# Fused substitution steps, joint weight-tile factors and a new instruction order in a one-core hybrid encoder kernel

## The chip, the cores and the metric

The kernel runs on one core of one Trainium2 chip. The metric is the device time of one execution in microseconds (us). Five engines work side by side, each through its own list of instructions in a fixed order: TensorE (PE in the profile; PEld are its weight loads), VectorE (DVE), ScalarE (ACT), GpSimd (POOL) and SyncE (SP), which issues the DMA transfers. An engine waits when the next instruction in its list needs something that another engine hasn't finished.

## The reference

One layer of an encoder trunk, over a prompt of 2048 frames and a second sequence of 32 frames with caches; the model is 1024 wide. Both sequences go through the same steps:

```python
h = layer_norm(x)
qa, ka, va, za, qkv_b, zb, a_b, b_b, gate_a, gate_b = split(h @ w_in)
ya = (band_attention(qa, ka, va, rel_bias) * silu(za)) @ w_branch_a      # 8 heads of 64, band of 9 chunks of 64
q, k, v = split(silu(causal_conv(qkv_b, conv_w)))                        # width 4
ob, state = gated_delta_rule(l2(q) / 8, l2(k), v, g(a_b), sigmoid(b_b), state)
yb = (rms_norm(ob) * gdn_norm_w * silu(zb)) @ w_branch_b
y = layer_norm(ALPHA * h + (sigmoid(gate_a) * ya + sigmoid(gate_b) * yb) @ w_out)
```

The delta rule runs over chunks of 64 frames. For each chunk and head a unit lower triangular system has to be inverted, and the state is carried from chunk to chunk:

```python
m = (k_beta @ k.T) * decay * strict                   # strictly lower triangular, 64x64
t_inv = triangular_solve(eye + m, eye)                # lower, unit diagonal
u, w = t_inv @ v_beta, t_inv @ (k_beta * exp(gc))
v_new = u - w @ s                                     # the chain: each chunk needs the state s before it
o = (q * exp(gc)) @ s + qk @ v_new
s = s * exp(g_last) + k_dec.T @ v_new
```

## The kernel before

The prompt is worked on in two halves of 1024 frames; the 32 sampled frames go along with the second. Each half has a delta-rule stage (branch B, `phase_b`) and an attention stage (branch A, `phase_a`); the branch products, the merge and the output projection come after, in part beside the second attention stage. Heads are taken in pairs of 128 partitions.

**Projections.** `w_in` is cut into 49 tiles of 128 columns. A tile is fetched (`wraw`), scaled by a power of two found from its squares, and divided into two half-precision parts (`whi`, `wlo`); `h` is kept in the same way (`hi`, `lo`). A projection block `pj` is 8 + 8 + 8 matmuls of 512 or 272 columns into one of two PSUM banks, and an eviction by ACT or DVE frees the bank (`raw`, `zb`, `vf`, `sig` and others). Since the scaling has to be undone, `factors` computes two numbers per tile, `w_inv` and `w_half`, from `w_scale` on DVE; evictions read them as scalars.

**Delta stage.** A half has 8 blocks (4 head pairs, twice 8 chunks), the second half one more for the sampled frames: 17 systems. For each block DVE and ACT compute a convolution (`acc` from `raw`, or from `raws` for the sampled frames), norms and decays; `system` makes the matrices `p_c` (the masked products, times the factor `e_p`) on PE and DVE; `solve` sends their 32x32 diagonal blocks through DRAM into `sys_p`, 128 systems side by side on the partitions, and `substitute` inverts them on DVE in 31 steps: step j takes column j times the rows known so far (`sys_t`) and subtracts it (`sys_u`). Only rows j // 4 + 1 of 8 are touched, so early steps are short. Two solvers run at a time. `inverse` brings the result back (`tu`, `tu_t`) and fills in the off-diagonal 32x32 blocks with matmuls (`z_c` between them). The state chain (`chain`) then takes for each chunk: PE x<-state, DVE r, PE x<-r, DVE vn, PE x<-vn, DVE state; beside it PE makes o<-state and o<-vn, which ACT copies into `v_t`. `tail` norms and gates a finished block (`sqo`, `ms`, `gb`) and stores it (`g`).

**What sets the order.** The program is written by generators, one for each stream of work. A planner (`Flow`) runs the one whose clock is earliest, and every instruction is appended to its engine's list as it is called. `Engine.price` gives each instruction a duration, `Flow.spend` books it: an engine is taken from its last booking, or a hop after the stream's last step, whichever is later (0.10 us into PE, 0.12 us on the same engine, 0.20 us between others). So the numbers in `price` decide the order of all five lists, and where among the projections the steps of the chain lie. On the chip there is no planner: the lists are fixed, and only semaphores hold an engine back.

Every instruction of the planned engines is recorded at one line, that of the call inside `Engine` (L267 before, L279 after), so the profile is read by names of tiles, not by lines. The lines of the old planner that the change touches:

```python
if a[1].dtype == F16:
    return max(n / 2400.0, m / 4800.0)
if a[1].dtype == F32R:
    return n / 2400.0
return max(n, m) / (1200.0 if name == "transpose" else 600.0)
...
return (0.05 if far else 0.093) + 0.093 * more + n / 1200.0
...
return (0.125 if far else 0.068) + 0.06 * more * fast + n / (1920.0 if fast else 960.0)
```

Here n is the width in elements, m that of the stationary operand, `far` is true where an operand lies in PSUM, `more` counts operands that are read as one scalar per partition, and `fast` is true for copies and TENSOR_SCALAR in SBUF. The last two lines are ACT and DVE.

## Time and profile before

| | before |
|---|---|
| median of 3 runs | 1968.77 us (1964.63 to 1972.47) |
| the profiled execution | 1967.06 us |
| its span, first to last instruction | 1965.2 us |
| PE busy | 1894.8 us (96%) |
| DVE busy | 1409.0 us (72%) |
| ACT busy | 993.6 us (51%) |
| POOL busy | 771.2 us (39%) |
| mean granted PE clock | 0.989 |
| DMA queue, share of 16 engines | 51.9% |

PE's busy time is a union of its matmuls, whose ends are modelled and which overlap, so 96% says that PE hardly stands still, not that it runs at its peak. DVE's share is an average: the profile's slices show it at 7 to 9 tenths in the delta stages, which lie at about 98 to 491 us and 884 to 1277 us, and at 4 to 7 tenths for most of the rest.

The kinds of rows that are read below: a row of a wait names the engine and the tile that waited, what was waited for, the time in total, the number of waits and the longest; a row of a group has the busy time and the mean duration in ns behind the bar, and then the idle time before it; a row in order of time has its start and its length in us.

### The profile page before, as it was taken

What the parts mean: (1) busy time and instruction counts of PE and PEld (TensorE: products, weight loads), DVE (VectorE), ACT (ScalarE), POOL (GpSimd) and SP (SyncE); (2) the same over time, 40 slices, a digit from 0 to 9 for tenths busy, and PEclk for the clock granted to TensorE, in tenths of its full rate; (3) what the DMA queues carried; (4) which work ended last, traced back from release to release, by engine and by line L of the source; (5) the groups of instructions that cost most, each with busy time, mean ns of one, the idle gap of its engine ahead of it and who ended that gap; (6) DMA issues with size and microseconds to landing.
All of it is one profiled execution on the core that took longest, in us unless ns stands there. A gap on an engine that the chain in (4) does not pass through costs nothing. (4 is left out here: it accounts for less than half of the span.)

```text
span 1965.2 us, 40968 instructions
## 1 busy us (share of the span) xinstructions
PE 1894.8 (96%) x14513; PEld 1339.0 (68%) x14513; DVE 1409.0 (72%) x4401; ACT 993.6 (51%) x2022; POOL 771.2 (39%) x1079
## 2 busy tenths in 40 slices
PE   8999999999999998999999999999999999999998
PEld 5445666676455556666776777768877667988886
DVE  7689989973378768679898987355556565465797
ACT  6665545544586777565544444354446575321110
POOL 7344334433344445444344333422222233243673
PEclk9999999999999999999999999999999999999999
DMA  3234232333368887223233233477878798996552
GB/s 134 69 89 114 78 108 68 84 90 105 115 154 203 179 185 168 75 81 84 58 79 93 67 91 103 120 206 189 223 190 172 184 198 187 263 331 200 179 183 89
DMA packets 382950, 274.61 MB, mean 140 GB/s; under 512 B 248339, under 2 KB 319359, under 8 KB 382745
## 3 DMA queue, kind: packets, MB, share of 16 engines
q1 hardware_dynamic: 382744, 272.00, 51.9%
q8 instruction: 114, 1.87, 0.4%
q14 instruction: 92, 0.75, 0.1%
HBM read 157.15 MB, written 71.76 MB: 116 GB/s over the span
## 5 line engine op out<-in xcount | busy, mean ns | idle before, releaser
L267 PE MATMUL pj<-hi,whi 128*128 128x512 f16 (+2 forms) x1992 | 643.0, 338 | 11.6 <-DVE zb L267 3.1
L267 PE MATMUL pj<-hi,wlo 128*128 128x512 f16 (+2 forms) x1952 | 634.5, 338 | 0.6 <-POOL wlo L267 0.5
L267 PEld LDWEIGHTS <-whi 128*128 128x128 f16 x3984 | 408.8, 104 | 229.0 <-issue 9.6
L267 POOL TENSOR_TENSOR wlo<-wraw,whi 128x256 f16<-128x256 f32 (+1 forms) x392 | 281.4, 740 | 466.9 <-ACT whi L267 380.7
L267 PE MATMUL pj<-lo,whi 128*128 128x512 f16 (+2 forms) x1992 | 453.0, 338 | 0.0
L267 PEld LDWEIGHTS <-wlo 128*128 128x128 f16 x1952 | 204.9, 105 | 116.2 <-issue 13.2
L267 ACT ACTIVATE sb<-sb,mx,unit 128x640 f32<-128x640 f32 (+4 forms) x128 | 108.6, 849 | 101.1 <-DVE mx L267 96.0
L267 POOL TENSOR_TENSOR pu<-sb,pu 128x640 f16<-128x640 f32 (+2 forms) x64 | 82.2, 1284 | 177.6 <-ACT pu L267 135.5
L267 ACT ACTIVATE wraw<-wraw,w_scale 128x1024 f32<-128x1024 f32 (+1 forms) x98 | 111.4, 1137 | 78.1 <-DVE w_scale L267 75.8
L267 ACT CAST whi<-wraw 128x512 f16<-128x512 f32 (+2 forms) x212 | 128.2, 611 | 28.0 <-PE pj L267 24.9
L267 DVE TENSOR_TENSOR sys_u<-sys_u,sys_t 128x60 f32<-128x60 f32 (+24 forms) x527 | 124.8, 242 | 5.7
L267 DVE SCALAR_TENSOR_TENSOR acc<-raw,cwT,acc 128x512 f32<-128x512 f32 x144 | 112.4, 781 | 7.9 <-ACT acc L267 6.5
L267 DVE TENSOR_TENSOR sys_t<-sys_u,sys_p 128x60 f32<-128x60 f32 (+21 forms) x459 | 110.6, 244 | 5.5
L267 ACT CAST mh<-sf 128x256 fp32r<-128x256 f32 x64 | 25.7, 406 | 158.3 <-PE c L267 78.1
L267 ACT COPY v_t<-o 128x64 f32<-128x64 f32 x132 | 27.7, 210 | 142.1 <-PE o L267 105.5
L267 DVE CUSTOM_DVE_ANT_0 sb<-a,bias 128x320 f32<-128x320 f32 (+5 forms) x136 | 66.2, 498 | 45.1 <-PE a L267 42.5
L267 POOL TENSOR_TENSOR w_scale<-w_scale,mhalf 128x1 f32<-128x1 f32 x49 | 32.0, 652 | 155.7 <-DVE w_scale L267 118.0
L267 PE MATMUL b<-ghi,whi 128*128 128x256 f32 (+1 forms) x320 | 89.3, 311 | 1.2 <-DVE cr L267 1.1
L267 POOL TENSOR_TENSOR ml<-sf,mh 128x256 fp32r<-128x256 f32 x60 | 59.5, 993 | 77.3 <-PE c L267 51.5
L267 ACT ACTIVATE sig<-pj,w_half 128x512 f32<-128x512 f32 (+2 forms) x84 | 49.3, 587 | 75.7 <-PE pj L267 70.3
L267 ACT CAST pu<-sb 128x640 f16<-128x640 f32 (+4 forms) x128 | 82.2, 650 | 0.7
L267 PEld LDWEIGHTS <-pt 128*128 128x128 f16 x1680 | 65.8, 98 | 23.3 <-issue 6.0
(389 smaller groups left out, 4202.9 us busy)
## 6 DMA issues: line engine op xcount, KB each, us to landing
wraw<-in_w_in SPq DMA_DIRECT2D x192, 256.0 KB
sf<-sig SPq DMA_DIRECT2D x112, 128.0 KB
sig<-sig SPq DMA_DIRECT2D x44, 256.0 KB
sg<-sig SPq DMA_DIRECT2D x37, 256.0 KB
sig<-sg SPq DMA_DIRECT2D x37, 256.0 KB
sys_p<-sol_p SPq DMA_DIRECT2D x68, 128.0 KB
x<-in_x_p SPq DMA_DIRECT2D x16, 512.0 KB
xt<-in_x_p SPq DMA_DIRECT2D x16, 512.0 KB
```

Source lines behind the costliest of these rows:

```text
L267: r = f(*a, **k)
```

## The change

There are four parts.

1. `Engine.price` gets other numbers. On PE half-precision matmuls cost 2.5 ns more, F32R ones some 5% and 6 ns more, and full-precision ones of 64 columns 0.168 us instead of 0.213. On ACT, operations of 1024 elements and half-precision ones out of PSUM on 64 partitions cost 0.13 us more. On DVE bn_aggr costs 0.16 more, TENSOR_TENSOR out of PSUM or on the substitution's rows 0.035 more, SCALAR_TENSOR_TENSOR of 512 elements 0.06 more in SBUF and 0.05 less out of PSUM. Nothing of this is executed; it moves instructions.
2. In `substitute`, steps with fewer than four rows use one SCALAR_TENSOR_TENSOR for each row (multiply by a scalar, then add, in place) instead of a multiplication into `sys_t` and a subtraction over all rows. All steps add instead of subtracting.
3. The sign that this needs is put into `e_p`, whose multiplication becomes a SCALAR_TENSOR_TENSOR with the constant -1; in turn `z_c` is a plain copy.
4. `w_inv` and `w_half` become the two columns of one tile `w_both`, written by one TENSOR_SCALAR (the two constants of `h_scale` times the reciprocal `w_one`) instead of two.

```diff
             if a[1].dtype == F16:
-                return max(n / 2400.0, m / 4800.0)
+                return max(n / 2400.0, m / 4800.0) + 0.0025
             if a[1].dtype == F32R:
-                return n / 2400.0
-            return max(n, m) / (1200.0 if name == "transpose" else 600.0)
+                return n / 2300.0 + 0.006
+            if name == "transpose":
+                return max(n, m) / 1200.0 + 0.002
+            if m <= 32:
+                return 0.064 + n / 1200.0 * (n > 32)
+            return max(n / 600.0, 0.112) + 0.006 + 0.05 * (n == HD)
...
-            return (0.05 if far else 0.093) + 0.093 * more + n / 1200.0
+            wide = 0.13 if n == KD * P or far and out.dtype == F16 and out.shape[0] == HD else 0.0
+            return (0.05 if far else 0.093) + 0.093 * more + n / 1200.0 + wide
...
+        if name == "tensor_tensor":
+            cost += 0.035 if far or len(out.shape) > 2 and out.shape[-1] < 32 and out.shape[0] == P else 0.0
+        if name == "scalar_tensor_tensor" and n == 512:
+            cost += -0.05 if far else 0.06
...
-        inv, half_ = w_inv[:, wid:wid + 1], w_half[:, wid:wid + 1]
-        V.reciprocal(out=half_, in_=w_scale[:, wid:wid + 1])
+        one = w_one[:, wid:wid + 1]
+        V.reciprocal(out=one, in_=w_scale[:, wid:wid + 1])
         yield
-        V.tensor_scalar(out=inv, in0=half_, scalar1=h_scale[:, 2:3], scalar2=None, op0=ALU.mult)
-        V.tensor_scalar(out=half_, in0=half_, scalar1=h_scale[:, 3:4], scalar2=None, op0=ALU.mult)
+        V.tensor_scalar(out=w_both[:, wid], in0=h_scale[:, 2:4], scalar1=one, scalar2=None, op0=ALU.mult)
...
-            V.tensor_tensor(out=e_p[:, 0:nch], in0=e_in[:, 0:nch], in1=bcast(s_p, nch), op=ALU.mult)
+            V.scalar_tensor_tensor(out=e_p[:, 0:nch], in0=e_in[:, 0:nch], scalar=-1.0, in1=bcast(s_p, nch),
+                                   op0=ALU.mult, op1=ALU.mult)
...
-                if nr == 1:
-                    V.tensor_scalar(out=sys_t[:, 0, 0:w], in0=sys_p[:, j, j + 1:32], scalar1=sys_u[:, 0, j:j + 1],
-                                    scalar2=None, op0=ALU.mult)
-                else:
-                    V.tensor_tensor(out=sys_t[:, 0:nr, 0:w], in0=sys_u[:, 0:nr, j:j + 1].to_broadcast([P, nr, w]),
-                                    in1=sys_p[:, j:j + 1, j + 1:32].to_broadcast([P, nr, w]), op=ALU.mult)
+                if nr < 4:
+                    for r in range(nr):
+                        u = sys_u[:, r, j + 1:32]
+                        V.scalar_tensor_tensor(out=u, in0=sys_p[:, j, j + 1:32], scalar=sys_u[:, r, j:j + 1], in1=u,
+                                               op0=ALU.mult, op1=ALU.add)
+                    yield
+                    continue
```

**DVE, the first steps of a substitution.** The first system's steps from a width of 31 columns on, before:

```order
L267 TENSOR_SCALAR sys_t<-sys_p,sys_u 128x31
L267 TENSOR_TENSOR sys_u<-sys_u,sys_t 128x31
L267 TENSOR_SCALAR sys_t<-sys_p,sys_u 128x30
L267 TENSOR_TENSOR sys_u<-sys_u,sys_t 128x30
L267 TENSOR_SCALAR sys_t<-sys_p,sys_u 128x29
L267 SCALAR_TENSOR_TENSOR acc<-raw_1426,cwT,acc 128x512
L267 TENSOR_TENSOR sys_u<-sys_u,sys_t 128x29
```

and with the change (x2 means two such rows in a line):

```order
L279 SCALAR_TENSOR_TENSOR sys_u<-sys_p,sys_u 128x31
L279 SCALAR_TENSOR_TENSOR acc<-raw_1437,cwT,acc 128x512
L279 SCALAR_TENSOR_TENSOR sys_u<-sys_p,sys_u 128x30
L279 SCALAR_TENSOR_TENSOR acc<-raw_1437,cwT,acc 128x512
L279 SCALAR_TENSOR_TENSOR sys_u<-sys_p,sys_u 128x29
L279 TENSOR_TENSOR sc<-gcb,col 128x8
L279 SCALAR_TENSOR_TENSOR sys_u<-sys_p,sys_u 128x28
L279 TENSOR_SCALAR ss<-b 64x8 x2
L279 SCALAR_TENSOR_TENSOR sys_u<-sys_p,sys_u 128x27 x2
```

One row stands for what were two, and from 27 columns on two or three rows for two; the 512-wide convolution steps of other streams now lie between them.

**PE, one step of the state chain.** Chunk step 65 (counted from 0 over both halves), the projections (`pj`) between x<-r and x<-vn, before:

```order
L267 MATMUL x<-r,u_bd_9736 128x64
L267 LDWEIGHTS wlo
L267 MATMUL pj<-hi_9067,wlo 128x512
L267 MATMUL o<-state,q_bd_9730 128x64
L267 LDWEIGHTS whi
L267 MATMUL pj<-hi_9067,whi 128x512
L267 MATMUL x<-vn,kd_bd_9733 128x64
```

and with the change:

```order
L279 MATMUL x<-r,u_bd_9692 128x64
L279 LDWEIGHTS whi
L279 MATMUL pj<-hi_9039,whi 128x512
L279 MATMUL o<-state,q_bd_9686 128x64
L279 LDWEIGHTS wlo
L279 MATMUL pj<-hi_9039,wlo 128x512
L279 LDWEIGHTS whi
L279 MATMUL pj<-lo_9040,whi 128x512
L279 LDWEIGHTS whi
L279 MATMUL pj<-lo_9040,whi 128x512
L279 MATMUL x<-vn,kd_bd_9689 128x64
```

Four projections stand where two stood.

**DVE, in front of one eviction.** The ninth eviction of a 512-wide `zb` block, which frees a projection bank early in the second half, before:

```order
L267 TENSOR_TENSOR q_bd_9731<-qk_10219,ex 64x8x64
L267 TENSOR_TENSOR sys_u<-sys_u,sys_t 128x6x10
L267 SCALAR_TENSOR_TENSOR acc<-raws_10830,cwT,acc 128x32
L267 TENSOR_TENSOR q_bd_9731<-qk_10219,ex 64x8x64
L267 TENSOR_TENSOR sys_t<-sys_u,sys_p 128x6x9
L267 SCALAR_TENSOR_TENSOR acc<-raws_10830,cwT,acc 128x32
L267 SCALAR_TENSOR_TENSOR zb<-zb,pj 128x512
```

and with the change:

```order
L279 SCALAR_TENSOR_TENSOR acc<-raw_10818,cwT,acc 128x512
L279 TENSOR_TENSOR sys_t<-sys_u,sys_p 128x6x8
L279 TENSOR_TENSOR kd_bd_9690<-b,sc 64x4x64
L279 SCALAR_TENSOR_TENSOR acc<-raw_10818,cwT,acc 128x512
L279 TENSOR_TENSOR sys_u<-sys_u,sys_t 128x6x8
L279 TENSOR_TENSOR kd_bd_9690<-b,swap 64x4x64 x2
L279 SCALAR_TENSOR_TENSOR acc<-raw_10818,cwT,acc 128x512
L279 TENSOR_TENSOR sys_t<-sys_u,sys_p 128x7x7
L279 SCALAR_TENSOR_TENSOR zb<-zb,pj 128x512
```

The q_bd steps and the convolution of the sampled frames have gone from in front of it, and the three steps of a 512-wide convolution and three kd_bd steps stand there.

17 lines of the change are left out of this document (11 added, 6 removed).

## The prediction

> **What bounds the kernel now.** I read the page's busy times first, then the stretches of the span, then what the matmul engine waited for.
>
> ```profile
> span 1965.2 us, 40968 instructions
> PE 1894.8 (96%) x14513; PEld 1339.0 (68%) x14513; DVE 1409.0 (72%) x4401; ACT 993.6 (51%) x2022; POOL 771.2 (39%) x1079
> ```
>
> PE is busy for 1894.8 of 1965.2 us. The change leaves PE's own work alone (the same matmuls but for three more warm-up ones on ones at the start), so only the 70.4 us in which PE stands still, and the clock it gets, can be won. The columns here are the stretch, its length, then each engine's busy time (instructions), then PE's clock and the DMA share.
>
> ```profile
> 0.00:40.00 40.00, 31.42 (x165) 17.92 (x165) 31.06 (x105) 23.96 (x50) 26.14 (x36) 0.91 0.44 153
> 98.00:293.00 195.00, 184.42 (x1277) 115.36 (x1276) 172.08 (x596) 108.73 (x207) 82.66 (x146) 0.98 0.35 98
> 293.00:491.00 198.00, 193.68 (x1512) 132.98 (x1513) 147.24 (x597) 93.40 (x199) 74.97 (x121) 1.00 0.31 86
> 491.00:884.00 393.00, 381.41 (x2856) 224.65 (x2855) 265.47 (x819) 275.40 (x521) 167.47 (x233) 1.00 0.60 145
> 884.00:1081.00 197.00, 186.94 (x1558) 136.55 (x1555) 179.26 (x640) 97.04 (x211) 76.44 (x140) 0.97 0.30 79
> 1081.00:1277.00 196.00, 191.92 (x1697) 146.48 (x1697) 139.71 (x557) 84.77 (x201) 69.14 (x114) 1.00 0.35 95
> 1277.00:1670.00 393.00, 384.08 (x3454) 292.66 (x3453) 229.27 (x709) 217.27 (x443) 112.27 (x121) 1.00 0.80 194
> 1867.00:1965.00 98.00, 90.09 (x392) 71.50 (x390) 83.57 (x106) 9.90 (x30) 53.18 (x52) 0.98 0.41 136
> ```
>
> PE's idle time is length minus PE busy: 8.6 us in the start, 29.1 in the two delta-rule halves (10.6 + 4.3 + 10.1 + 4.1), 20.5 in the two attention stages (11.6 + 8.9), 7.9 at the end; the rest, 4.1, is in stretches not shown. In the first part of each half DVE is busy for 172.08 of 195 and 179.26 of 197 us: it is the engine that PE waits for there.
>
> ```profile
> PE x L267 <- DVE vn L267: 6.1, 16, 0.8
> PE c L267 <- DVE ob L267: 4.6, 5, 1.4
> PE b L267 <- ACT p_c L267: 3.8, 2, 3.2
> PE x L267 <- DVE r L267: 3.7, 11, 1.1
> PE pj L267 <- DVE zb L267: 3.1, 1, 3.1
> PE o L267 <- ACT v_t L267: 2.7, 6, 0.7
> PE x L267 <- DVE sys_u L267: 1.8, 2, 1.1
> PE b L267 <- DVE kd_bd L267: 1.5, 1, 1.5
> PE b L267 <- POOL v_t L267: 1.5, 2, 1.4
> PE x L267 <- DVE state L267: 1.1, 4, 0.5
> ```
>
> No wait is longer than 3.2 us; these rows alone hold fifty. The recurrent chain (the rows of x and o) makes 6.1 + 3.7 + 2.7 + 1.8 + 1.1 = 15.4 us. The other rows of the delta halves (p_c, zb, kd_bd, v_t on POOL) make 3.8 + 3.1 + 1.5 + 1.5 = 9.9 us.
>
> **How such a wait arises.** One of them, in order of time (start, length in us):
>
> ```profile
> 951.15 0.67 DVE L267 TENSOR_TENSOR q_bd<-qk,ex 64x512 f32<-64x512 f32 x1
> 951.75 0.66 DVE L267 TENSOR_TENSOR sys_u<-sys_u,sys_t 128x28 f32<-128x28 f32 x1
> 952.33 0.27 DVE L267 TENSOR_SCALAR vn<-x,sc 128x64 f32<-128x64 f32 x1
> 952.66 0.43 PE L267 MATMUL x<-vn,kd_bd 128*128 128x64 f32 x2 [0.33 <-DVE vn L267]
> ```
>
> PE had two projection matmuls to do between x<-r and x<-vn; DVE had q_bd and a sys_u step in front of vn, and that sys_u took 0.66 us where its group's mean is 0.24 (row below). So part of a wait is a plan that is too tight, and part a duration that no fixed number foresees. The change can only reach the first.
>
> **The chain's order.** At the place shown in the section on the change, x<-r to x<-vn holds four projections instead of two. Counted over all steps, that hop holds 4.6 projections on average instead of 3.3, and at most three of them in 70 of 128 steps instead of 85 of 126. The other hops hardly change: state to r, at most three in 67 instead of 64; vn to state, 86 instead of 96. So short hops fall from 245 to 223, by a tenth, and by a fifth on the hop that waits most. Eight projections of this width take 1.89 us here, 0.22 us each:
>
> ```profile
> 1264.98 1.89 PE L267 MATMUL pj<-lo,whi 128*128 128x512 f16 x8
> ```
>
> Waits grow with the shortage, so I take a third of the chain's 15.4 us, **5 us**; bounds 0 and 12.
>
> **The other waits in the delta halves.** The dearer numbers for wide DVE and ACT operations push the planner to start dependants later. But in front of zb the new DVE order holds three 512-wide acc steps instead of two short ones, so this wait may well return. I take 40% of 9.9 us, **4 us**; bounds 0 and 8.
>
> **Attention stages.** Numbers of ACT casts and of DVE evacuations change by 0.05 to 0.13 us, and the order with them; of 20.5 us I take **3 us**; bounds -5 (new waits) and 10. Start and end keep their order nearly: **0**.
>
> **The substitution steps.**
>
> ```profile
> L267 DVE TENSOR_TENSOR sys_u<-sys_u,sys_t 128x60 f32<-128x60 f32 (+24 forms) x527 | 124.8, 242 | 5.7
> L267 DVE TENSOR_SCALAR sys_t<-sys_p,sys_u 128x31 f32<-128x31 f32 (+1 forms) x68 | 19.8, 291 | 0.3
> L267 DVE SCALAR_TENSOR_TENSOR acc<-raws,cwT,acc 128x32 f32<-128x32 f32 x36 | 10.4, 288 | 2.3 <-ACT acc L267 1.9
> L267 DVE SCALAR_TENSOR_TENSOR qk_s<-e,acc 128x32 f32<-128x32 f32 x8 | 1.5, 186 | 0.6 <-ACT e L267 0.6
> L267 DVE TENSOR_SCALAR w_inv<-w_half,h_scale 128x1 f32<-128x1 f32 x49 | 10.0, 204 | 0.5
> ```
>
> In each of 17 systems the first twelve steps lose 24 instructions (4 TENSOR_SCALAR, 20 TENSOR_TENSOR) and gain 24 fused ones (4 + 4 x 2 + 4 x 3), at most 31 wide. Removed: 4 x 0.291 + 20 x 0.242 = 6.0 us a system. Added: by the nearest row of the same kind (acc on raws, 32 wide, a scalar read per partition, adding in place) 24 x 0.288 = 6.9 us; by qk_s, whose scalar is a constant, 24 x 0.186 = 4.5 us. So DVE gains 1.5 us or loses 0.9 us per system, over 17 systems 26 us won to 15 us lost. I take the acc row, being the same form, less the overlap of rows that don't wait for each other: about nothing. The joint factor saves one 128x1 TENSOR_SCALAR for each of 49 tiles, 10.0 us of DVE by its row. The turned sign in e_p and the plain copy of z_c stay in instructions that were there. DVE isn't the bound, so none of it is PE time by itself: **0**.
>
> **The clock.** After some waits PE gets half its clock for one or two periods:
>
> ```profile
> core 0: 1965.2 us, clock 0.989
> 136.90:140.00 3.10, 0.01 (x1) 0.02 (x1) 3.06 (x11) 2.63 (x6) 3.10 (x3) 1.00 0.02 6
> 142.10:145.50 3.40, 3.40 (x11) 1.60 (x10) 3.32 (x13) 0.00 (x0) 0.99 (x1) 0.50 0.43 136
> 168.80:170.30 1.50, 0.20 (x1) 0.00 (x0) 1.44 (x4) 1.11 (x3) 0.36 (x1) 1.00 0.10 37
> 172.80:176.20 3.40, 3.40 (x11) 1.72 (x10) 3.02 (x19) 2.76 (x4) 2.91 (x3) 0.51 0.00 0
> ```
>
> A stop of 3.1 us at 137 and one of 1.3 us at 169 are each followed by 3.4 us at half clock, which costs 1.7 us of work. The mean clock of 0.989 makes some 20 us lost in all. If about two such periods go with the waits, **4 us**; bounds -3 and 10. The Trainium skill (TensorE: Matmul & The Clock Gate, "Why this matters for your kernels") advises against idle gaps over about 3 us; by that rule only the longest waits cost clock, this term would be under 2 us, and the sum 2 us less. The row at 172.8, behind a gap of 1.3 us, speaks against so high a threshold.
>
> **The ends of the halves.** The chain now ends nearer to the attention's first projection: 32 instead of 98 wide projections stand between them in the first half, and some 6.9 instead of 18.0 us of them in the second (6 and 48 of 512 and 272 columns, instead of 32 and 96). What follows the chain there now:
>
> ```profile
> 1241.47 0.33 PE L267 MATMUL o<-vn,qk_bd 128*128 128x64 f32 x2
> 1255.80 1.25 SPq L290 DMA_DIRECT2D g<-gb  x2
> 1266.90 0.69 ACT L267 ACTIVATE vf<-pj,w_inv 128x512 f32<-128x512 f32 x1 [3.53 <-PE pj L267]
> ```
>
> The last block's norm, gate and store end at 1257.1, 15.3 us behind the chain, and the first eviction of attention at 1266.9. With 11 us less between them that tail would end some 1 to 2 us after the eviction could begin; the second bank covers most of it: **-1 us**.
>
> **The sum.** 5 + 4 + 3 + 0 + 4 - 1 = 15 us. The profiled execution took 1967.06 us, 1.9 more than its span and 1.7 less than the median of 1968.77. So 1967 - 15 = **1952 us**. With the upper bounds (12 + 8 + 10 + 10) it would be 1927.
>
> **The rivals.** *The waits move.* Waits by scatter (the sys_u of 0.66 us) stay as many and stand elsewhere. For it: fifty small waits, short hops down by only a tenth, and the old order's luck is lost with its faults. Against it: the hop that waits most is the one that was widened. Time 1967, give or take 6.
>
> *DVE falls behind: slower.* The planner charges a fused step of 31 columns 0.10 us and a hop of 0.12 to the next on the same engine, 0.22. If on the chip each holds DVE for the whole 0.288 us of the acc row, it lags 24 x 0.07 = 1.6 us a system, 28 us in all, where DVE has only 23 and 18 us to spare in the first parts of the halves, and every chain step queues behind it. If half of it reaches PE and the other gains fail, 1967 + 14 = 1981. It decides once a fused step holds DVE for more than about 0.25 us. Against it: two or three fused steps in a row don't wait for each other, and above vn and the next acc start 0.20 us apart though vn takes 0.27, so independent instructions overlap.
>
> **How the numbers follow.** A measurement of this kernel can tell about 0.5% from no change. Forecast (some waits go) 0.53; waits move 0.31; DVE falls behind 0.16. Hence faster by over 0.5% 0.53, within it 0.31, slower 0.16. The range runs from 1932, near the upper bounds of the gains, to 1977, which leaves out the worse half of the slow case.
>
> **What would show it.** Right: PE idle near 59 us instead of 70, the waits for vn and r below 7 us together (now 9.8), the mean clock at 0.99 or above, PE's busy time shorter by the clock term alone. The fused steps: their row's mean between 0.19 and 0.29 us; above it the slow case. The second half's end: a wait of pj for vf near its end. Wrong: the same idle sum under other names, or idle grown most where DVE was fullest, after 98 and after 884 us.

## The result and the profile after

The changed kernel takes 1978.43 us (median of 6 runs, 1975.52 to 1982.23), the kernel before 1967.91 us in the runs beside it (6 runs, 1964.63 to 1972.47). The ratio is 1.0054, 95% interval 1.004 to 1.0067: slower by half a per cent where 0.8% faster was forecast. In a second measurement of the same kernel (e10 below) it was 1.0038 [1.0025, 1.0051]. The profiled execution took 1975.9 us, its span 1974.1 us, 8.9 more than before, at a mean clock of 0.987 (0.989 before).

The head of the page of the changed kernel:

```profile
span 1974.1 us, 40895 instructions
PE 1884.3 (95%) x14516; PEld 1344.8 (68%) x14516; DVE 1403.9 (71%) x4352; ACT 990.8 (50%) x2022; POOL 768.8 (39%) x1079
```

PE's idle time rose from 70.4 to 89.8 us, its busy time fell by 10.5. The stretches, with the columns of before (stretch, length, busy time of PE, PEld, DVE, ACT and POOL, PE clock, DMA share and rate):

```profile
0.00:40.00 40.00, 29.42 (x168) 17.28 (x168) 34.43 (x102) 22.38 (x47) 25.86 (x36) 1.00 0.41 141
40.00:98.00 58.00, 55.02 (x331) 30.36 (x332) 35.15 (x74) 37.58 (x62) 23.47 (x34) 0.94 0.21 68
98.00:293.00 195.00, 184.74 (x1263) 113.67 (x1262) 171.80 (x577) 109.60 (x208) 89.00 (x149) 0.98 0.35 97
293.00:491.00 198.00, 193.11 (x1542) 136.25 (x1542) 147.90 (x589) 95.21 (x203) 71.64 (x117) 1.00 0.31 87
491.00:884.00 393.00, 376.12 (x2817) 222.17 (x2816) 261.81 (x804) 270.51 (x515) 163.90 (x230) 0.99 0.60 145
884.00:1081.00 197.00, 188.42 (x1635) 143.33 (x1633) 179.05 (x635) 98.89 (x216) 76.77 (x140) 0.98 0.30 82
1081.00:1277.00 196.00, 192.28 (x1703) 148.93 (x1702) 140.91 (x571) 85.19 (x199) 72.11 (x121) 0.99 0.35 97
1277.00:1670.00 393.00, 379.03 (x3389) 286.99 (x3387) 229.10 (x703) 216.28 (x445) 110.73 (x121) 0.99 0.79 191
1670.00:1769.00 99.00, 89.10 (x728) 82.19 (x726) 50.99 (x92) 30.82 (x63) 32.48 (x31) 0.95 0.91 283
```

Length less PE busy: the delta halves stand still for 27.5 us (10.3 + 4.9 + 8.6 + 3.7; 29.1 before), the attention stages for 30.9 (16.9 + 14.0; 20.5 before), the start for 10.6 + 3.0 (8.6 + 0.2 before), and 1670 to 1769, where the merge begins, for 9.9 (3.0 before). So by idle time the loss isn't where DVE is fullest, but where the forecast expected little or nothing. What PE waited for (waiting tile, what was waited for, us in total, number, longest):

```profile
PE c L279 <- DVE ob L279: 9.3, 4, 6.6
PE b L279 <- ACT whi L279: 7.3, 5, 3.2
PE x L279 <- DVE r L279: 5.3, 8, 2.4
PE x L279 <- DVE vn L279: 4.8, 9, 0.8
PE pj L279 <- ACT part L279: 3.8, 1, 3.8
PE a L279 <- ACT mh L279: 3.7, 1, 3.7
...
PE pj L279 <- DVE zb L279: 1.1, 2, 0.9
```

Before, no wait was longer than 3.2 us. Now ob has one of 6.6, part one of 3.8 and mh one of 3.7, none of them in a delta half (that of part is at the opening of the second attention stage). The waits for r and vn are 10.1 us together (9.8 before), zb's fell from 3.1 to 1.1.

**A better measure than idle time.** PE's idle time misses part of what PE loses, as these rows in order of time show (changed kernel; start, length):

```profile
622.66 0.38 PE L279 MATMUL pj<-lo,whi 128*128 128x512 f16 x1
622.88 0.38 PE L279 MATMUL pj<-hi,whi 128*128 128x512 f16 x1
```

Each record lasts 0.38 us, but the next matmul starts after 0.22. A matmul that starts 0.16 us late leaves no idle time at all. So I took, for every matmul, the time to the start of the next one, less the median of that spacing in the kernel before, taken where two matmuls of its kind (same tiles, same shape) follow each other. The medians add up to 1773.0 us in both kernels (warm-up matmuls left out), so PE's own work is the same, and what is left over is called lost time. Its level hangs on this choice: with medians over all successors, a change from one kind to another counts as work, PE's own work is 1835.0 us, and 62 us less is lost in every kernel. The differences between kernels stay the same within 0.1 us.

The table adds the lost time up over the matmuls, cut at 65, 410, 780, 1122 and 1495 us of PE work, so that the same work is compared; the kernel before gets there at 96, 491, 881, 1277 and 1670 us, the edges of its stages. One profiled execution each, ratios from all runs of a kernel against before; cells are us lost. The column of the chains is the work from 150 to 440 and from 840 to 1120 us (193 to 521 and 951 to 1275 us in the kernel before), which holds nearly all steps of the state chains and leaves out the first part of each half. The us that the expectations of e5 and e16 to e18 give for the delta halves are of this last kind.

| run | ratio, 95% interval | start | half 1 | att. 1 | half 2 | att. 2 | merge, end | all | halves 1 + 2 | chains |
|---|---|---|---|---|---|---|---|---|---|---|
| before | 1 | 31.2 | 49.3 | 20.6 | 53.5 | 20.2 | 9.1 | 183.9 | 102.8 | 82.6 |
| changed | 1.0054 [1.0040, 1.0067] | 37.0 | 44.0 | 27.0 | 43.0 | 27.1 | 14.8 | 192.8 | 87.0 | 71.4 |
| e10 changed, again | 1.0038 [1.0025, 1.0051] | 37.3 | 41.5 | 26.9 | 42.7 | 28.9 | 16.1 | 193.4 | 84.2 | 71.6 |
| e1 new prices only | 1.0015 [1.0004, 1.0027] | 36.0 | 42.5 | 30.6 | 33.9 | 31.0 | 15.1 | 189.1 | 76.4 | 61.2 |
| e2 edits, old prices | 1.0000 [0.9987, 1.0013] | 32.2 | 59.4 | 21.1 | 53.1 | 15.9 | 12.4 | 194.0 | 112.5 | 94.9 |
| e3 edits, order held | 1.0033 [1.0020, 1.0046] | 30.0 | 52.8 | 17.7 | 58.8 | 19.5 | 9.3 | 188.0 | 111.6 | 93.3 |
| e4 new order, old steps | 1.0135 [1.0119, 1.0152] | 36.1 | 53.3 | 28.7 | 50.8 | 27.9 | 15.5 | 212.3 | 104.1 | 86.3 |
| e5 new prices in delta halves | 0.9967 [0.9955, 0.9979] | 34.6 | 48.9 | 24.9 | 37.2 | 26.9 | 11.1 | 183.5 | 86.1 | 69.5 |
| e6 new prices elsewhere | 1.0110 [1.0092, 1.0129] | 31.5 | 60.7 | 21.7 | 56.0 | 23.7 | 14.9 | 208.6 | 116.7 | 100.1 |
| e7 = e5 with the edits | 0.9965 [0.9950, 0.9980] | 32.3 | 46.4 | 22.1 | 42.6 | 23.2 | 10.5 | 177.1 | 89.0 | 75.4 |
| e8 prices of PE only | 1.0074 [1.0049, 1.0100] | 34.6 | 54.5 | 27.1 | 44.8 | 24.6 | 9.4 | 195.1 | 99.3 | 78.9 |
| e9 = e7, gate blocks later | 0.9980 [0.9967, 0.9993] | 34.0 | 44.9 | 27.6 | 41.0 | 20.7 | 10.9 | 179.1 | 85.9 | 73.5 |
| e11 before, LEAD nudged | 1.0006 [0.9995, 1.0017] | 30.0 | 53.0 | 22.3 | 51.0 | 18.1 | 10.5 | 184.9 | 104.0 | 83.6 |
| e12 before, hop nudged | 1.0014 [1.0001, 1.0027] | 29.8 | 50.8 | 21.9 | 52.3 | 19.2 | 11.4 | 185.5 | 103.2 | 83.7 |
| e13 changed, norm earlier | 1.0067 [1.0047, 1.0087] | 35.6 | 41.2 | 30.3 | 42.5 | 28.7 | 17.4 | 195.7 | 83.8 | 71.2 |
| e14 changed, gate blocks later | 1.0037 [1.0021, 1.0053] | 36.6 | 49.2 | 27.6 | 43.1 | 26.2 | 13.4 | 196.3 | 92.4 | 76.4 |
| e15 prices of ACT only | 1.0113 [1.0089, 1.0137] | 38.0 | 58.1 | 27.4 | 52.3 | 19.6 | 13.9 | 209.4 | 110.4 | 95.3 |
| e16 prices of DVE only | 1.0019 [1.0001, 1.0038] | 31.6 | 52.2 | 29.2 | 37.0 | 25.7 | 12.7 | 188.4 | 89.2 | 84.0 |
| e17 = e7, LEAD nudged | 1.0005 [0.9992, 1.0018] | 32.3 | 45.5 | 26.0 | 39.7 | 24.3 | 12.3 | 180.0 | 85.2 | 72.2 |
| e18 = e7, hop nudged | 1.0004 [0.9991, 1.0016] | 33.8 | 46.6 | 23.2 | 41.4 | 30.5 | 11.7 | 187.2 | 88.0 | 74.1 |

The first two rows tell the result: the changed kernel wins 15.8 us in the delta halves (5.3 + 10.5) and loses 5.8 in the start, 6.4 + 6.9 in the attention stages and 5.7 in the merge and at the end, 8.9 in all, the difference of the spans. The row of e10, a second execution of the same kernel, shows that a cell comes back within 2.5 us, half of them within 0.5. Other runs repeat parts of an order and show more scatter: e13 and e14 have the changed kernel's order up to 577 and 1275 us, and half 1 takes 41.2 and 49.2 there; e9 has that of e7 up to 1267 us, and att. 1 takes 27.6 and 22.1. So a single cell can be off by some 5 us, while the sums over the halves and over the rest (87.0 and 105.8 changed, 84.2 and 109.2 in e10, 102.8 and 81.1 before) stand clear of that. Single executions of one kernel lie up to 0.5% from its median, so whole times are read from the ratios alone. The profiled one of e2 is such a one (1977.07 us where the median of its runs is 1967.63), and its cells are too high by some 9 us together.

Outside the halves 24.7 us more are lost. The three longest waits, 14.1 us together, lie there, and these are their places. **First attention stage, about 617 to 637 us.** Columns as in the stretches above; changed kernel:

```profile
617.00:637.00 20.00, 13.62 (x119) 7.67 (x117) 19.60 (x56) 14.83 (x27) 9.84 (x12) 0.96 1.06 235
```

and DVE there in order of time (x and mv are the layer norm of the second half's frames, vmax and part serve the next head pair's v and k, ob is the attention's output on its way out of PSUM):

```profile
634.16 0.80 DVE L279 TENSOR_SCALAR x<-x,mv 128x1024 f32<-128x1024 f32 x1
...
635.28 1.40 DVE L279 SCALAR_TENSOR_TENSOR part<-pj,kst 64x512 f16<-64x512 f32 x2
636.72 0.47 DVE L279 TENSOR_SCALAR ob<-c,rs 128x64 f32<-128x64 f32 x2
```

and what PE did (start, length, and in brackets the wait before it):

```profile
637.24 0.80 PE L279 MATMUL c<-vt,pt 128*128 128x64 f16 x12 [6.62 <-DVE ob L279]
```

DVE is full for 20 us: the norm now falls together with a head pair's v and k (11 of its larger operations, 7.9 us, lie in them). The same 20 us before, and the 20 us in which the norm lay then, when DVE was as full and PE stood still for 2.9 us:

```profile
600.00:620.00 20.00, 17.14 (x112) 8.92 (x110) 19.56 (x65) 11.73 (x25) 8.63 (x13) 0.91 0.76 228
617.00:637.00 20.00, 20.00 (x124) 10.11 (x123) 14.85 (x49) 15.19 (x26) 6.38 (x7) 0.93 0.65 146
```

**Second attention stage, at 1275 us.** DVE, then ACT, of the changed kernel (glo is the lower part of the gate blocks' division for the branch products):

```profile
1275.27 1.41 DVE L279 SCALAR_TENSOR_TENSOR part<-pj,kst 64x512 f16<-64x512 f32 x2 [15.44 <-ACT kst L279]
1276.71 2.16 DVE L279 TENSOR_TENSOR glo<-glo,ghi 128x256 fp32r<-128x256 f32 x2
1278.79 1.74 DVE L279 TENSOR_REDUCE vmax<-vf 128x1 f32<-128x1536 f32 x1
```

```profile
1280.95 0.72 ACT L279 ACTIVATE part<-vf,vsc 128x512 f16<-128x512 f32 x1 [0.48 <-DVE vsc L279]
1282.96 0.49 ACT L279 ACTIVATE part<-pj,w_both 128x272 f32<-128x272 f32 x1 [1.28 <-DVE part L279]
```

Before, glo started at 1274.15 and vmax at 1275.59, ahead of DVE's part<-pj, and ACT's part did not wait for vsc. Now the bank that part<-pj frees at 1283 stands behind glo, vmax and vsc, and PE waits 3.8 us.

**Merge, at 1705 us.** SP's queue, changed kernel, then DVE:

```profile
1704.69 5.50 SPq L302 DMA_DIRECT2D sl<-sig  x4
...
1710.71 0.43 SPq L302 DMA_DIRECT2D sf<-sig  x1
```

```profile
1715.56 0.42 DVE L279 TENSOR_TENSOR sf<-sf 128x256 f32<-128x256 f32 x1 [4.57 <-DMA sf<-sig]
```

The loads of sl stand in front of the first load of sf, which the merge's mh comes from, four where there were three. Their row is 5.50 us long because SP stands still within it, as its own waits from 1704 to 1710 us say, changed kernel and then before:

```profile
SPq L302 <- DMA g<-ga: 3.7, 1, 3.7
```

```profile
SPq L290 <- DMA g<-ga: 1.2, 1, 1.2
```

The second load of sl has to wait until the store of a gate block (g<-ga) has landed, 3.7 us instead of 1.2, and everything behind it in SP's list waits too; the load that was added takes less than 0.5. So sf is issued at 1710.71 instead of 1708.79, while PE is ready for its first product with mh at 1712.82 instead of 1714.22. It waits 3.7 us instead of 0.5.

### The profile page after: what moved, and what is told of

It is laid out like the page before. It is cut to its first block, busy times and chain, and to the rows that moved or that the text cites. A ratio compares the mean times of both kernels' runs of the same rounds, so it can differ in the third digit from the quotient of the medians.

```text
span 1974.1 us, 40895 instructions
## 1 busy us (share of the span) xinstructions
PE 1884.3 (95%) x14516; PEld 1344.8 (68%) x14516; DVE 1403.9 (71%) x4352; ACT 990.8 (50%) x2022; POOL 768.8 (39%) x1079
## 5 line engine op out<-in xcount | busy, mean ns | idle before, releaser
L279 PEld LDWEIGHTS <-wlo 128*128 128x128 f16 x1952 | 205.2, 105 | 116.3 <-issue 14.9
L279 ACT ACTIVATE wraw<-wraw,w_scale 128x1024 f32<-128x1024 f32 (+1 forms) x98 | 111.3, 1136 | 85.3 <-DVE w_scale L279 77.7
L279 DVE SCALAR_TENSOR_TENSOR sys_u<-sys_p,sys_u 128x20 f32<-128x20 f32 (+11 forms) x408 | 98.0, 280 | 3.6 <-DMA sys_p<-sol_p 2.5
L279 ACT COPY v_t<-o 128x64 f32<-128x64 f32 x132 | 27.6, 209 | 139.0 <-PE o L279 110.7
L279 PE MATMUL b<-ghi,whi 128*128 128x256 f32 (+1 forms) x336 | 93.3, 310 | 1.3 <-ACT v_s L279 1.3
L279 PEld LDWEIGHTS <-pt 128*128 128x128 f16 x1680 | 66.3, 98 | 30.5 <-issue 9.3
L279 POOL TENSOR_TENSOR ml<-sf,mh 128x256 fp32r<-128x256 f32 x60 | 59.5, 993 | 69.0 <-PE c L279 37.5
L279 PE MATMUL b<-ghi,wlo 128*128 128x256 f32 (+1 forms) x336 | 83.8, 282 | 0.0
L279 PE MATMUL c<-vt,pt 128*128 128x64 f16 x1680 | 70.1, 194 | 11.4 <-DVE ob L279 9.3
```

The costliest lines, as they stand in the source:

```text
L279: r = f(*a, **k)
```

## The experiments

The first four part the change into its order and its instructions. Theory A: the order that the new numbers lay out loses. Rival B: the fused steps make DVE late. Rival C: every new order scatters by some 10 us.

**e1.**

```diff
             if a[1].dtype == F16:
-                return max(n / 2400.0, m / 4800.0)
+                return max(n / 2400.0, m / 4800.0) + 0.0025
...
```

> Only the new numbers of price; substitution, sign and factors as before. Theory A (the order that the new numbers lay out is what loses, 10.5 us of the whole change): ratio to before 1.004 to 1.007, PE idle 85 to 95 us instead of 70.4, with the growth again in the attention stages (30 us instead of 20.5) and the merge stretch. Rival B (the fused steps make DVE late): within 0.1% of before, idle near 70. Rival C (every new order scatters by some 10 us, nothing in the numbers themselves is bad): anywhere from 0.995 to 1.007, with other waits than the changed kernel has.

1.0015 [1.0004, 1.0027]: little of the loss, above B's bound, below A's, and inside C's wide one. The table shows why: 26.4 us won in the delta halves, 31.6 lost in the other stages. So A only in part: the new numbers do two opposite things. It also means that the edits aren't free in this plan. From e1 to the changed kernel the ratio rises from 1.0015 to 1.0054 (1.0038 in e10), and 8 to 11 us of the gain in the halves go (76.4 to 87.0 and 84.2 us lost). Whether that is the fused steps or the other order that comes with them, this pair of kernels doesn't say.

**e2.** The changed kernel, but in `price`:

```diff
             if a[1].dtype == F16:
-                return max(n / 2400.0, m / 4800.0) + 0.0025
+                return max(n / 2400.0, m / 4800.0)
...
```

> The changed kernel with the old numbers of price: fused steps, sign and joint factors, order planned anew by the old numbers. Theory A: within 0.15% of before. Rival B: ratio 1.004 to 1.007, with the waits for vn and r above 12 us together. Rival C: anywhere from 0.995 to 1.006, whatever e3 gives.

1.0000 [0.9987, 1.0013], as A has it. The gain of the delta halves is gone with the new numbers: 112.5 us lost there, 103 if all of the 9 us by which this execution is slow lie there, and 102.8 before.

**e3.** The changed kernel with the old numbers, and in `substitute` (the joint factor is treated alike):

```diff
...
                 if nr < 4:
                     for r in range(nr):
                         u = sys_u[:, r, j + 1:32]
-                        V.scalar_tensor_tensor(out=u, in0=sys_p[:, j, j + 1:32], scalar=sys_u[:, r, j:j + 1], in1=u,
-                                               op0=ALU.mult, op1=ALU.add)
+                        V.eng.scalar_tensor_tensor(out=u, in0=sys_p[:, j, j + 1:32], scalar=sys_u[:, r, j:j + 1], in1=u,
+                                                   op0=ALU.mult, op1=ALU.add)
+                    flow.spend("V", 0.128 + w / 1920.0 if nr == 1 else 0.068 + nr * w / 960.0)
+                    yield
+                    flow.spend("V", 0.068 + nr * w / 960.0)
                     yield
                     continue
```

> The fused steps, the sign and the joint factors, but booked in the planner at the price and the yields of the instructions that they replace, so that every other instruction stands where it stood before (the same lists on PE, POOL and SP). Prices the edits alone. Theories A and C: within 0.15% of before, 1965 to 1971 us; DVE busy within 15 us of 1409. Rival B: ratio 1.004 or more and the waits for vn and r up by 5 us.

1.0033 [1.0020, 1.0046], between the two, and the waits for r and vn at 12.7 us (7.7 + 5.0), 2.9 more than before. In this order, where the fused steps stand together in the place of the first of two, they cost something. The longest of these waits, of x for r, is 3.9 us; DVE, then POOL, in front of it (L1319 are the fused steps):

```profile
1192.19 0.55 DVE L267 TENSOR_TENSOR sys_t<-sys_u,sys_p 128x42 f32<-128x42 f32 x1
1192.67 1.94 DVE L1319 SCALAR_TENSOR_TENSOR sys_u<-sys_p,sys_u 128x23 f32<-128x23 f32 x3
1194.53 0.19 DVE L267 TENSOR_TENSOR sys_u<-sys_u,sys_t 128x42 f32<-128x42 f32 x1
1194.75 0.28 DVE L267 SCALAR_TENSOR_TENSOR r<-x,negc,v_t 128x64 f32<-128x64 f32 x1
```

```profile
1192.01 2.56 POOL L267 TENSOR_TENSOR wlo<-wraw,whi 128x256 f16<-128x256 f32 x4 [4.43 <-ACT whi L267]
```

Three fused steps in a row, which take 0.54 us (median), take 1.94 us beside POOL's subtraction, and r, which stands behind them, is late by 1.4 us for it. More on this at the end.

**e4.** The changed kernel, and the joint factor treated alike:

```diff
...
                 if nr < 4:
-                    for r in range(nr):
-                        u = sys_u[:, r, j + 1:32]
-                        V.scalar_tensor_tensor(out=u, in0=sys_p[:, j, j + 1:32], scalar=sys_u[:, r, j:j + 1], in1=u,
-                                               op0=ALU.mult, op1=ALU.add)
+                    if nr == 1:
+                        V.eng.tensor_scalar(out=sys_t[:, 0, 0:w], in0=sys_p[:, j, j + 1:32],
+                                            scalar1=sys_u[:, 0, j:j + 1], scalar2=None, op0=ALU.mult)
...
+                    V.eng.tensor_tensor(out=sys_u[:, 0:nr, j + 1:32], in0=sys_u[:, 0:nr, j + 1:32],
+                                        in1=sys_t[:, 0:nr, 0:w], op=ALU.add)
+                    for r in range(nr):
+                        flow.spend("V", 0.068 + w / 960.0)
                     yield
```

> The reverse: the order of the changed kernel on all engines, but in each place of the fused steps and the joint factor the two instructions that they replaced (multiply into sys_t, then add over all rows). Theories A and C: as slow as the changed kernel, ratio 1.004 to 1.007 to before, the wait of c for ob of 6 us at about 630 us and that of pj for part at about 1279 us still there. Rival B: back at before, within 0.15%.

1.0135 [1.0119, 1.0152], outside both ranges, and against B: with the old steps in the same order the kernel is slower still. The three long waits are there again at 6.6, 3.8 and 3.7 us, so no fused step causes them; and the chain waits are up:

```profile
PE x L279 <- DVE r L279: 10.3, 12, 3.2
...
PE x L279 <- DVE vn L279: 7.3, 10, 1.8
```

Two old steps, of which the second needs the first, take 0.46 us for one row of 30 columns, where the plan books 0.10 and a fused step takes 0.235. In this order the fused steps are worth 15 to 20 us (1.0135 against 1.0054 and 1.0038), 17.1 of them in the halves.

Theory D was formed on this: the new numbers help the delta halves and hurt everything else. The next three switch them by stage.

**e5.** The kernel before, with `price_new` the new function:

```diff
     def price(self, name, a, k):
+        if self.flow.fine:
+            return self.price_new(name, a, k)
...
         enter(1, half, make)
+        flow.fine = True
         flow.run(done)
+        flow.fine = False
```

> The kernel before with the new numbers of price used only while the two delta-rule halves are planned; start, attention and merge are planned by the old ones. Instructions as before. Theory D (the new numbers help the delta halves and hurt the start, the attention stages and the merge): by the profile of e1, whose delta halves took 7 and 15 us less beyond their matmuls' own time than before, 1947 to 1957 us, ratio 0.989 to 0.995, and the waits of c for ob, pj for part and a for mh as in before. Rival C (scatter of any new order, at no fixed place): anywhere from 0.996 to 1.006.

0.9967 [0.9955, 0.9979], faster than before, by less than D has it, and inside the range of C. The halves win 16.7 us of lost time (13.1 by the chains' column), but the second attention stage opens with a wait of pj for part of 5.7 us and loses 6.7, though its own numbers are the old ones, and the other stages lose 9.6 more.

**e6.** The same with the two values of `fine` exchanged.

> The complement of e5: the new numbers in the start, the attention stages and the merge, the old ones in the delta halves. Theory D: slower, 1980 to 1993 us, ratio 1.006 to 1.013, the delta halves as before, the loss in the start (5 us), at the start of each attention stage (4 to 7 us) and in the merge stretch (10 us). Rival C: anywhere from 0.996 to 1.006.

1.0110 [1.0092, 1.0129], the loss expected, but only in part at the places expected: 10.8 us in start, attention and merge (91.9 against 81.1), and 13.9 in the delta halves, which I had expected as before. The old numbers are worse there once what comes ahead is laid out differently.

**e7.** e5 made on the changed kernel.

> The changed kernel, new numbers only in the delta halves (e5 with the fused steps, the sign and the joint factors). Theory D, with the edits costing DVE time in the delta halves as e3 showed (0.33%): 1955 to 1964 us, slower than e5 by 4 to 10 us. If the edits are free in this order: level with e5.

0.9965 [0.9950, 0.9980], level with e5: in this plan the edits cost nothing.

**e8.** The kernel before:

```diff
...
-                return n / 2400.0
-            return max(n, m) / (1200.0 if name == "transpose" else 600.0)
+                return n / 2300.0 + 0.006
...
+            return max(n / 600.0, 0.112) + 0.006 + 0.05 * (n == HD)
```

> The kernel before with the new numbers for PE alone (half-precision, F32R and full-precision matmuls, transposes). If they are what moves the plan against the DMAs and so what hurts the start and the merge: idle up by 5 us or more before 98 us and after 1670 us, ratio 1.002 to 1.010. If the ACT and DVE numbers do it: those two places as before, ratio 0.995 to 1.002.

1.0074 [1.0049, 1.0100], the ratio that was expected if they hurt the start and the merge, but not the places: idle time grows by 2.9 us before 98 us and by 0.3 from 1670 to 1769 us. The start loses 3.4 us, the merge only 0.3, the attention stages 6.5 and 4.4, and the delta halves win 3.5.

**e9.** On e7:

```diff
-            for gen in (early_g(), early_sg(), early(), load_a(), merge()):
+            flow.start(early_g(), flow.cur.clock + 25.0)
+            for gen in (early_sg(), early(), load_a(), merge()):
                 flow.start(gen)
```

> e7 with one stream started 25 us later: the one that reads the finished gate blocks back and divides them for the branch products (ghi, glo). In e7 and in the changed kernel three of its glo subtractions stand on DVE in front of the maximum over v (vmax) at the start of the second attention stage, ACT waits for that, and PE 4.5 us for ACT's part. If this is the cause of the loss at that place: the wait of pj for part falls to 1.5 us or less, and the time to 1954 to 1959 us, 3 to 6 below e7 (ratio 0.992 to 0.995). If ACT's own load there is the cause: the wait stays over 3 us and the time level with e7 (0.9965).

The wait fell as expected, but 0.9980 [0.9967, 0.9993] is not better than e7. PE's waits from 1240 to 1320 us, e7 and then e9:

```profile
PE pj L313 <- ACT part L313: 4.5, 1, 4.5
PE b L313 <- DVE cr L313: 2.1, 1, 2.1
```

```profile
PE b L313 <- DVE cr L313: 3.8, 1, 3.8
PE pj L313 <- DVE ql L313: 1.6, 1, 1.6
PE pj L313 <- ACT part L313: 1.3, 1, 1.3
```

So the stream of the gate blocks was the cause at this place. That it is glo on DVE in front of vmax, and not its ghi casts on ACT, the run doesn't part, since both start later. Of the 3.2 us won, the next waits took back 2.5 (cr 1.7, ql 0.8). The second attention stage as a whole loses 20.7 us here, as before, but the sum over the halves and the other stages hardly changes from e7 to e9.

**e10.** The changed kernel once more.

> The changed kernel once more, to see which of its waits come back in a second execution. If the waits are set by the order: ob at about 630 us, part at about 1279 and mh at about 1712 again within 1 us each, ratio 1.004 to 1.007. If they are scatter of one execution: other places, same sum.

The order sets them: ob at 6.6, part at 3.8, mh at 3.4 us. Ratio 1.0038 [1.0025, 1.0051]; two measurements of one kernel can thus lie 0.16% apart.

**e11 and e12.** The kernel before:

```diff
-LEAD = 5.0
+LEAD = 5.05
```

```diff
-HOP_PE, HOP, HOP_SAME = 0.1, 0.2, 0.12
+HOP_PE, HOP, HOP_SAME = 0.101, 0.2, 0.12
```

> The kernel before with one planner constant moved by 1% (LEAD 5.0 to 5.05): another order without any reason in it. Sizes what a new order does by itself. Theory D: within 0.25% of before, with delta halves as before. Rival C: 0.3% or more off.

> The same with the hop into PE booked at 0.101 instead of 0.1 us. Theory D: within 0.25% of before. Rival C: 0.3% or more off.

1.0006 [0.9995, 1.0017] and 1.0014 [1.0001, 1.0027], the delta halves as before (104.0 and 103.2 us). But the traces show that these nudges move little: e11's instructions stand in another order almost only in the first attention stage, those of e12 almost only behind 1484 us, and neither moves one in a delta half. So they are no test of C for the halves, and C stays open.

**e13.** The changed kernel:

```diff
-AHEAD = 100.0
+AHEAD = 60.0
```

> The changed kernel with the stream that normalizes the second half's frames started 60 instead of 100 us after the first attention stage begins (AHEAD). If its bn_stats and x steps in front of ob on DVE cause the wait of 6.6 us of c for ob at about 630 us: no wait for ob over 3 us there, 4 to 6 us won, ratio to before 1.000 to 1.003. If ob is late for another reason: a wait of over 5 us for ob again, ratio 1.003 to 1.006.

The cause of this wait is confirmed, the gain isn't. From 540 to 760 us PE's longest wait for ob is now 2.3 us:

```profile
PE c L279 <- DVE ob L279: 3.7, 3, 2.3
```

The wait of 6.6 us is gone, yet pj waits 2.9 us for ql in its place, the ratio is 1.0067 [1.0047, 1.0087], above both ranges, and the first attention stage loses 30.3 us instead of 27.0.

**e14.** The edit of e9 on the changed kernel.

> The changed kernel with the gate blocks' stream started 25 us later, as in e9. The maximum over v then stands on DVE ahead of the glo subtractions at the start of the second attention stage. If that order causes the wait of pj for part (3.8 us): 1.5 us or less; time 1 to 4 us below the changed kernel if nothing comes back elsewhere, level with it if the casts only collide later, as in e9.

The wait for part is 1.8 us instead of 3.8, that for cr 3.2 instead of 1.9, and the time is level, 1.0037 [1.0021, 1.0053].

**e15 and e16.** The other two groups of numbers, each alone on the kernel before.

```diff
-            return (0.05 if far else 0.093) + 0.093 * more + n / 1200.0
+            wide = 0.13 if n == KD * P or far and out.dtype == F16 and out.shape[0] == HD else 0.0
+            return (0.05 if far else 0.093) + 0.093 * more + n / 1200.0 + wide
```

```diff
...
+        if name == "bn_aggr":
+            cost += 0.16
...
+        if name == "scalar_tensor_tensor" and n == 512:
+            cost += -0.05 if far else 0.06
```

> The kernel before with the new numbers for ACT alone. If they carry the loss of the start: 3 to 5 us more before 98 us than before, and delta halves within 6 us of before; ratio 1.000 to 1.006. If they carry the gain in the delta halves: 10 us or more less there.

> The kernel before with the new numbers for DVE alone. If they carry the gain in the delta halves, where DVE is the engine waited for: 8 us or more less there than before (82 us beyond the matmuls' own time), ratio 0.992 to 1.000. If not: within 6 us there, and the gain needs the three groups together.

ACT's numbers alone: 1.0113 [1.0089, 1.0137], the start worse by 6.8 us and the first half by 8.8. So ACT's numbers alone hurt the start as PE's do (3.4). DVE's alone: 1.0019 [1.0001, 1.0038]. The chains' column stands at 84.0 us, as before, but the halves as wholes lose 13.6 us less (89.2 against 102.8), nearly all of it in the second, and the other stages 18.1 more. The three groups alone cost 0.74, 1.13 and 0.19%, 2.06% together; all at once cost 0.15% (e1) and win 26.4 us in the halves, of which DVE's numbers alone win 13.6, PE's 3.5, while ACT's lose 7.6. The whole of the gain needs the set.

**e17 and e18.** e7 with the nudges of e11 and e12.

> e7 with LEAD 5.05 instead of 5.0 (the nudge of e11). If the gain belongs to the new numbers in the delta halves: ratio to before 0.994 to 0.9985, delta halves 68 to 77 us beyond the matmuls' own time (75 in e7, 83 before). If e7 was one lucky order: 0.9985 to 1.003, delta halves 80 us or more.

> e7 with the hop into PE booked at 0.101 us (the nudge of e12). The same two outcomes and bounds as for e17.

By the time, 1.0005 [0.9992, 1.0018] and 1.0004 [0.9991, 1.0016], the gain of e7 doesn't come back. By the chains (72.2 and 74.1 us) it does, but that says little: by the traces e17 has e7's order outside the first attention stage, but for a few instructions, and e18 has it in the first half. A nudge that moves almost nothing but one attention stage went with 0.4% of the time, nearly as much as the changed kernel's whole loss (and 0.16% can be the difference of two measurements). So e5 and e7 measured a third of a per cent below before, but that the new numbers in the halves give a faster kernel as a rule is not shown.

## Why the prediction was wrong

**What bounds the kernel** held: PE's own work is 1773.0 us before and after, and only lost time moved.

**Chain waits 5 and other waits of the delta halves 4:** right in sign, too small in sum. The halves lose 15.8 us less (102.8 to 87.0). In front of the matmuls of x, the chain's, the lost time falls by 8.4 (35.6 to 27.2), 5.5 of it in front of x<-vn (12.9 to 7.4), behind the hop that the new order widened; the rest, 7.4, is near the upper bound of the other waits. But it wasn't to be read where I had said: the rows for r and vn stayed at 10.1 us, since the chain's idle time hardly changed and the gain lies in what the overlapping records hide. By idle time the halves win only 1.6.

**Attention stages 3, bounds -5 to 10:** this step failed. Idle there grew by 10.4 us and lost time by 13.3, beyond the bound. I treated 20.5 us of waits as a stock that a better plan draws down. But the old order happened to have the second half's norm, the gate blocks and the pairs' v and k side by side with little collision, and a new order deals these out afresh. There was more to lose than to win at places where nothing waited.

**Start and end 0, since they "keep their order nearly":** failed too: 5.8 us lost in the start (6.1 in the second execution) and 5.7 in the merge and at the end. I counted a changed order only on PE; that SP's queue would stand behind the landing of g's store for 3.7 us, in front of sf, I had not looked at.

**The ends of the halves -1:** right in kind, too small. All of e5, e7, e17 and e18, with old numbers in attention, lose 3 to 10 us more than before in the second attention stage, and e9 shows a cause at the opening: the finished gate blocks come to ACT and DVE just when vmax is due. The wait of pj for vf that I had named didn't come (0.2 us); the one for part, a few us later, did.

**The fused steps 0:** right for DVE's time, not shown for the kernel's. Their mean is 280 ns, inside the range named, by the first row

```profile
L279 DVE SCALAR_TENSOR_TENSOR sys_u<-sys_p,sys_u 128x20 f32<-128x20 f32 (+11 forms) x408 | 98.0, 280 | 3.6 <-DMA sys_p<-sol_p 2.5
L279 DVE TENSOR_TENSOR sys_t<-sys_u,sys_p 128x60 f32<-128x60 f32 (+17 forms) x323 | 77.7, 241 | 3.2
L279 DVE TENSOR_TENSOR sys_u<-sys_u,sys_t 128x60 f32<-128x60 f32 (+17 forms) x323 | 76.2, 236 | 3.4
L279 DVE TENSOR_SCALAR w_both<-h_scale,w_one 128x2 f32<-128x2 f32 x49 | 15.6, 318 | 0.5
```

98.0 + 77.7 + 76.2 = 251.9 us for the substitutions, against 124.8 + 110.6 + 19.8 = 255.2 before. The joint factor takes 15.6 us in place of w_inv's 10.0 and a like row for w_half (10.5), so it saves 4.9, not 10.0. By e2 and e7 the edits are free, by e3 they cost 0.33% in an order that isn't made for them, and from e1 to the changed kernel 0.23 to 0.39% in one that is.

**The clock 4:** wrong in sign. The mean fell from 0.989 to 0.987; the stretches at half clock add up to 47.6 us instead of 37.5, which is 5 us of work and part of the lost time above. Over all executions of the measurement of e10 the mean is 0.9856 (5 executions) against 0.9885 (30 of the kernel before), so an estimate from these is 0.0029 x 1970 = 5.7 us, most of the kernel's net loss. Three of the stretches follow the new stops, 6.8 us behind the wait for ob and 3.4 each behind those for part and mh. The first of them:

```profile
635.30:642.10 6.80, 4.86 (x23) 2.26 (x23) 3.53 (x10) 2.56 (x6) 2.32 (x2) 0.50 0.95 210
```

Two others, from 1051.7 and from 1099.5 us, follow no stop at all, and both come back in e10 (1048.9 and 1096.7). In the 3.4 us before the second, PE shows no idle time, but 32 of its 45 matmuls there are 2 columns wide, 16 in the row shown and 16 more from 1098.40:

```profile
1096.10:1099.50 3.40, 3.40 (x45) 2.99 (x45) 2.31 (x8) 0.68 (x3) 0.00 (x0) 0.99 0.65 169
1099.50:1102.90 3.40, 3.40 (x17) 2.72 (x18) 2.04 (x11) 2.65 (x7) 1.93 (x3) 0.50 0.01 1
1096.99 1.09 PE L279 MATMUL b<-sel,p_c 128*64 128x2 f32 x16
```

The prediction's reading of the row at 172.8 as "behind a gap of 1.3 us" needs the same care: the stop ends at 170.52, 1.5 us long, and 16 matmuls of 2 columns follow it for 1.06 us.

**The rivals.** That DVE falls behind through the fused steps is not what happened: with the old steps in the same order the kernel is slower still (e4). "The waits move" is nearest to what happened, but I had it as an even exchange, 1967 give or take 6. It was not even: 15.8 us come out of the halves, and 24.7 go into stages that had had fewer collisions.

What stays open is how much of this belongs to the new numbers and how much to the luck of an order. The halves speak for the numbers: three orders that the old ones laid out there lose 102.8, 112.5 (e2, whose execution was a long one) and 116.7 us (e6), four by the new ones 76.4 to 89.0 (e1, e5, changed, e7). The rest does too: 81.1 and 81.5 us where all is laid out by the old numbers (before, e2), 105.8 and 112.7 where all is by the new ones (changed, e1). But these are few orders, and the net, 0.15 to 0.5%, is no larger than what a nudge went with in e17. Why the merge and the start come out worse is open as well. In every kernel whose merge was planned by all the new numbers it loses 13 to 17 us (9 to 12 with all the old ones there), but which number does it was not tried, and by e13, e9 and e14 the mending of one wait needn't win anything.

## What to carry to other kernels

When a change lays out the whole order afresh, count what each stage can lose as well as what it can win: a stage without waits is one whose transfers and casts happen not to collide, and a new plan deals them again. Measure such a plan stage by stage, at equal amounts of the bounding engine's work and by start-to-start spacing, since the whole time hides a gain of 16 us behind a loss of 25. And removing a long wait is no gain by itself: three times here (e9, e13, e14) one went or was halved, and the time stayed or rose. When a nudge is to show what a new order does by itself, count first how many instructions it moves, and where.

## What the hardware showed that I had not expected

**DVE stands still beside POOL.** In the rows of e3 above, DVE's operations between 1192.2 and 1194.5 us start within POOL's four subtractions (2.56 us together) and end with them; a fused step takes 0.235 us (median) when POOL is idle and up to 0.75 beside it. It depends on what POOL does: in the changed kernel a fused step that starts beside a subtraction of wlo takes 0.65 us (median of 46), one beside POOL's rr<-ss,expo, 8 columns wide and 1.7 us long, 0.235 (39). Taking for every DVE operation that starts beside a POOL operation its time less the median of its kind with POOL idle, DVE loses 95.3 us before and 99.9 in the changed kernel, 38 of them in the substitutions in both. What the prediction called "a duration that no fixed number foresees", the sys_u of 0.66 us, is of this kind (a subtraction of wlo runs from 951.70 to 952.37 us), and no number of `price` can have it, since it depends on what POOL does. The Trainium skill (SBUF — State Buffer, "SBUF: two separate sides") says that DVE with two SBUF inputs and a GpSimd operation that reads SBUF take a shared pair of ports whole, and that the later one "fully blocks"; the rows of wlo agree, with 1.94 us for three steps that otherwise take 0.54, those beside rr don't.

**PE's recorded ends overlap the next start** by 0.16 us for matmuls of 512 columns, so idle time can miss what PE loses: 70.4 us idle in the kernel before, against 183.9 lost by spacing, or some 122 if changes of kind count as work. Both hold the half-clock stretches and all of the start too.

**Half clock can follow narrow matmuls.** The two stretches at half clock from 1051.7 and 1099.5 us, shown above for the second, come behind 3.4 us without idle time in which rows of 16 matmuls of 2 columns take 2.2 us.
